# A scan and the subtraction behind it as one step of the plan

## The chip, the cores and the metric

The kernel runs on one core of a Trainium2 chip. The metric is the device time of one execution in microseconds (us), as the median of several runs. The core's engines work side by side, each through its own list of instructions in a fixed order: TensorE (PE in the profile, with PEld for its weight loads), VectorE (DVE), ScalarE (ACT), GpSimd (POOL) and SyncE (SP), which issues most DMAs. They wait for each other through semaphores.

## The reference

The model is a two-layer decoder trunk on 256 tokens of width 1024. Layer 0 is stick-breaking attention with 16 heads of 64, then an MLP with squared ReLU. Layer 1 is sparse attention with shared keys and values, then another such MLP. The change touches the attention of layer 0 alone:

```python
z = jnp.einsum('bqhd,bshd->bhqs', q_blk, k).astype(jnp.float32) * scale
causal = key_pos[None, :] < t[:, None]
log_1m = jnp.where(causal, jax.nn.log_sigmoid(-z), 0.0)
excl = lax.cumsum(log_1m, axis=3, reverse=True) - log_1m
a = jnp.where(causal, jnp.exp(jax.nn.log_sigmoid(z) + excl), 0.0)
return jnp.einsum('bhqs,bshd->bqhd', a.astype(v.dtype), v)
```

The weight of a key is therefore exp(z minus the sum, over this key and all later ones up to the query, of log(1 + exp z)). The sum runs from the last key back to the first.

## The kernel before

The kernel is one long program, written out instruction by instruction. The order of the matmuls on PE is given by hand. The order of the small work on DVE, ACT and POOL is chosen by a planner (class `Order`) while the program is built. It keeps a clock of its own. Each matmul that is written out advances the clock by an assumed cost. Small work is given to it as chains (class `Chain`), generators that yield one step after another. A step is a dictionary from the engines that could do it ("D", "A", "G" for DVE, ACT, POOL) to an assumed cost in ns, the function that issues the instruction, and a flag for a port that DVE and POOL share. When an engine is free by the planner's clock, it takes the step with the lowest rank among those that are ready. The next step of a chain becomes ready 35 ns after the end of the last by that clock, so between two steps of one chain another chain's step can take the engine. What `need` asks for must be planned before the next matmul is written.

Every fp32 weight is split into two parts for PE. ACT casts the raw tile to `wh` (line 422) and DVE subtracts that from it to get `wl` (line 437). A raw tile whose `wl` is done can be loaded anew by SP.

The attention of layer 0 handles eight pairs of heads in four groups g of two pairs. `proj(p)` multiplies the queries and keys of pair p into PSUM tiles `qk`. ACT copies one part to `qku` (1037), DVE adds the other into `qkT` (1038), and DVE or POOL multiplies by the row scale (1040, 1041). `scores(g)` multiplies `qkT` into `z`, in PSUM banks 4 to 7, and starts a chain `soft` for each pair. That chain is:

- DVE caps `z` into `sbe`, two halves (1052);
- ACT takes the exponential (1056) and the logarithm of one plus it (1057) into `sbs`;
- DVE sums `sbs` backwards with a scan (1058);
- DVE subtracts `sbs` from `sbe` (1059);
- ACT takes the exponential of `sbe` (1060).

`turn(g, i, b)` transposes four tiles of 128 by 128 of `sbe` on PE into bank b (`pa`), and ACT or DVE copies them to `sbt` (1097). `values(g, b)` multiplies `sbt` with `v` into `po` in bank b, and `o_evac` brings it to `oT` in two parts: a cast on ACT (649) and a subtraction on DVE (650). `out_part` multiplies `oT` with the output weights into the accumulators `acc`.

PE's order in a group g from 1 on is: a part of `proj(2g+2)` with the transposes of group g-1 in between, `scores(g)`, `values(g-1)`, the rest of `proj(2g+2)` and `proj(2g+3)`. Behind the last of these come `out_part` for the first heads, the transposes of group 2, `scores(3)`, `values(2)`, and further parts of the output projection. `values(2, 1)` puts its `po` in bank 1, and the accumulator `acc11`, which is written next but a few matmuls, takes bank 1 as well.

In this text the groups are counted from 1: group 1 is `scores(0)`, and group 4 is `scores(3)`.

Of the kernel before, what the change touches and what calls it, by code (L numbers as in the profile page):

```python
# [12 lines left out]
OP = mybir.AluOpType  # L13
# [3 lines left out]
D = 1024  # L17
# [148 lines left out]
def act(n, f, more=0):  # L166
    return {"A": (195 + 0.835 * n + more, f, False)}


def dve(n, f, more=0, port=False):  # L170
    return {"D": (150 + 1.045 * n + more, f, port)}
# [7 lines left out]
def hybrid_kernel(ctx, tc, x, xt, eye, gcols, gfin, wqk, wv, wo0, wkv, wvs, wq, wg, wo1, w1, w2, cw1, cw2, cpos, gate_b, consts, out):  # L179
    nc = tc.nc  # L180
# [731 lines left out]
    def layer0(ap):  # L912
# [76 lines left out]
        go_on = ap.tile([P, 2 * ROW], BF16, name="go_on", bufs=1)  # L989
# [56 lines left out]
        def soft(z, got):  # L1046
            e = ap.tile([P, 2 * ROW], F32, name="sbe", bufs=3)
            s = ap.tile([P, 2 * ROW], F32, name="sbs", bufs=2)
            nc.gpsimd.memset(e.rearrange("p (b c) -> p b c", b=6)[:, :, P:SEG], NEG)

            def low(hd):
                return dve(384, lambda: nc.vector.tensor_tensor(
                    e[:, hd * ROW:(hd + 1) * ROW].rearrange("p (b c) -> p b c", b=3)[:, :, 0:P],
                    z[hd][:, 0:384].rearrange("p (b c) -> p b c", b=3), cap, op=OP.min))
            yield [low(0), low(1)]
            yield act(774, lambda: nc.scalar.activation(s, e, AF.Exp))
            yield act(774, lambda: nc.scalar.activation(s, s, AF.Ln, bias=1.0))
            yield dve(774, lambda: nc.vector.tensor_tensor_scan(s[:, ::-1], s[:, ::-1], go_on[:, ::-1], 0.0, OP.add, OP.mult), 810, True)  # L1058
            yield {"D": (956, lambda: nc.vector.tensor_sub(e, e, s), True)}
            yield act(774, lambda: nc.scalar.activation(e, e, AF.Exp))  # L1060
            got.append(e)

        def scores(g):
            zs = [[B(4 + 2 * j + hd, "z") for hd in range(2)] for j in range(2)]
            qks = []
            for j in range(2):
                qkT, ch = live.pop(("q", 2 * g + j))
                o.need(*ch)
                qks.append(qkT)
            o.tick(90)  # L1070
            for j in range(2):
                for hd in range(2):
                    r = slice(hd * DH, (hd + 1) * DH)
                    mm(zs[j][hd][:, 0:256], qks[j][r, 0, P:2 * P], qks[j][r, 1, :], True, False, 2.0)
                for hd in range(2):
                    r = slice(hd * DH, (hd + 1) * DH)
                    mm(zs[j][hd][:, 256:384], qks[j][r, 0, 0:P], qks[j][r, 1, 0:P], False, True, 2.0)
                got = []
                live["e", 2 * g + j] = got, go(soft(zs[j], got), 1 + 0.01 * g)
            o.tick(90)  # L1080
# [893 lines left out]
```

## Time and profile before

| | us |
|---|---|
| median of 3 runs | 591.42 |
| lowest and highest | 591.16, 592.12 |
| the profiled execution | 591.92 |
| its span, first to last instruction | 590.1 |
| PE busy in it | 581.5 |
| DVE busy | 523.6 |
| ACT busy | 433.3 |
| POOL busy | 94.6 |

The profiled execution is one run of the program. The table's busy times are sums over the span. A busy PE is not a PE at its peak, because matmuls are pipelined and their ends are modelled. In rows of the trace the first number is the start in us from the start of the span and the second the duration. A row ending in "x3" holds three such instructions one behind the other. A bracket names the idle time of the engine just before, and whose work ended it.

### The profile page before, as it was taken

Reading aid. Unit: us, or ns where it says so; the run is one execution under the profiler, and the core shown is the slowest. Engines: PE = TensorE matmul, PEld = TensorE weight load, DVE = VectorE, ACT = ScalarE, POOL = GpSimd, SP = SyncE. Lnnn points to the kernel's source line nnn. Section 1 sums busy time; section 2 is a strip of 40 time slices with the busy share of each in tenths; the row PEclk is TensorE's granted clock in tenths of the full one; section 3 lists DMA queues with packets and bytes.
Section 4 is the critical chain, followed back from the end, with each engine's and each line's share of the span. In section 5 each row is a group of like instructions: output and inputs, shape, how many; then the busy total and the mean of one; then the engine's idle time right before and its main releaser. Section 6 shows DMA issues by size and latency. Waiting matters only on the chain.

```text
span 590.1 us, 9338 instructions
## 1 busy us (share of the span) xinstructions
PE 581.5 (99%) x3340; PEld 487.7 (83%) x3340; DVE 523.6 (89%) x842; ACT 433.3 (73%) x704; POOL 94.6 (16%) x114
## 2 busy tenths in 40 slices
PE   9999999999999999999999999999999999999995
PEld 6888887888888888888888878677888888888884
DVE  6679999699999999987895899965999999999976
ACT  6757776588797878783944797572988988887863
POOL 0013220001211212000120443330001121211001
PEclk9999999999999999999999999999999999999998
DMA  8982337179888998544645634323399888987311
GB/s 325 402 283 76 124 127 264 66 236 387 271 207 241 276 293 248 163 140 150 202 165 182 250 110 139 113 107 108 110 366 333 206 271 228 315 256 202 69 37 71
DMA packets 38063, 119.77 MB, mean 203 GB/s; under 512 B 4608, under 2 KB 5888, under 8 KB 38016
## 3 DMA queue, kind: packets, MB, share of 16 engines
q1 hardware_dynamic: 31248, 106.94, 51.1%
q0 software_dynamic: 6336, 11.54, 11.8%
q10 hardware_dynamic: 432, 0.69, 0.3%
q8 instruction: 26, 0.43, 0.3%
q14 instruction: 21, 0.17, 0.1%
HBM read 118.10 MB, written 1.05 MB: 202 GB/s over the span
## 4 chain that ended last, share of the span: by engine, by line
PE 88%; DVE 7%; ACT 4%; issue 1%; POOL 0%; POOLq 0%; ACTq 0%
PE acc L554 32%; PE pu L554 30%; PE pk L554 5%; PE qk L554 4%; PE pv L554 4%; PE qp L554 3%; PE po L554 3%; DVE wl L437 2%; PE z L554 2%; PE ptp L566 2%; DVE sbs L1058 1%; ACT pe L1462 1%; PE ph L554 1%; ACT wh L422 1%; PE pt L566 1%
## 5 line engine op out<-in xcount | busy, mean ns | idle before, releaser
L437 DVE TENSOR_TENSOR wl<-raw,wh 128x1024 fp32r<-128x1024 f32 x128 | 157.4, 1246 | 8.6 <-ACT wh L422 7.7
L422 ACT CAST wh<-raw 128x1024 fp32r<-128x1024 f32 x128 | 132.8, 1054 | 18.3 <-DMA raw<-in_wq 6.9
L554 PE MATMUL pu<-xn,wh 128*128 128x512 f32 x512 | 126.9, 390 | 0.0
L554 PEld LDWEIGHTS pu<-xn,wh 128*128 128x128 f32 x512 | 95.2, 188 | 19.2
L554 PEld LDWEIGHTS pu<-xn,wl 128*128 128x128 f32 x512 | 68.4, 188 | 5.0
L554 PE MATMUL pu<-xn,wl 128*128 128x256 f32 x512 | 69.4, 278 | 0.0
L444 POOL DMA_DIRECT2D fours<-in_w x24 | 22.4, 933 | 196.3 <-DVE ms L802 101.8
L769 ACT COPY mu<-pu 128x512 f32<-128x512 f32 x64 | 37.2, 583 | 16.6 <-PE pu L554 16.1
L554 PE MATMUL acc<-wh,hh 128*128 128x512 f32 (+1 forms) x126 | 49.3, 392 | 0.0
L554 PE MATMUL acc<-wl,hh 128*128 128x512 f32 (+1 forms) x126 | 49.2, 390 | 0.0
L554 PE MATMUL acc<-wh,hl 128*128 128x512 f32 (+1 forms) x126 | 48.8, 387 | 0.0
L554 PE MATMUL acc<-wh,oT 128*128 128x512 f32 x128 | 43.5, 402 | 0.7 <-DVE oT L650 0.7
L554 PE MATMUL acc<-tl,hh 128*128 128x512 f32 x104 | 40.8, 392 | 0.0
L554 PE MATMUL acc<-th,hh 128*128 128x512 f32 x104 | 40.7, 392 | 0.0
L554 PE MATMUL acc<-th,hl 128*128 128x512 f32 x104 | 40.5, 389 | 0.0
L791 DVE TENSOR_TENSOR hl<-ms,hh 128x896 fp32r<-128x896 f32 (+2 forms) x34 | 33.1, 978 | 5.7 <-ACT hh L790 5.7
L785 ACT ACTIVATE ms<-ms 128x512 f32<-128x512 f32 x32 | 20.2, 633 | 24.0 <-DVE ms L784 23.8
L444 POOL DMA_DIRECT2D four<-in_w x20 | 18.9, 946 | 87.3 <-DVE ms L802 13.9
L790 ACT CAST hh<-ms 128x896 fp32r<-128x896 f32 (+2 forms) x34 | 29.0, 854 | 5.1 <-DVE ms L802 3.5
L1462 ACT ACTIVATE pe<-pe,nm 128x256 f32<-128x256 f32 (+1 forms) x64 | 28.5, 450 | 5.7 <-DVE nm L1460 5.7
L554 PE MATMUL pk<-wh,xk 128*128 128x512 f32 (+1 forms) x128 | 32.6, 339 | 0.0
L554 PE MATMUL qk<-xa,wh 128*128 128x512 f32 x128 | 31.2, 393 | 0.0
(229 smaller groups left out, 1239.8 us busy)
## 6 DMA issues: line engine op xcount, KB each, us to landing
raw<-in_w SPq DMA_DIRECT2D x76, 512.0 KB, 7.3
four<-in_w SPq DMA_DIRECT2D x28, 512.0 KB, 7.4
fours<-in_w SPq DMA_DIRECT2D x24, 512.0 KB, 8.2
raw<-in_wqk SPq DMA_DIRECT2D x16, 512.0 KB, 6.2
raw<-in_wo SPq DMA_DIRECT2D x16, 512.0 KB, 4.7
fours<-in_w POOLq DMA_DIRECT2D x24, 256.0 KB, 7.2
four<-in_w POOLq DMA_DIRECT2D x20, 256.0 KB, 6.6
raw<-in_wkv SPq DMA_DIRECT2D x8, 512.0 KB, 3.9
```

Of the source, the lines that this page charges most:

```text
L422: k = {"A": (195 + 0.835 * m, lambda: nc.scalar.copy(a, b), False), "D": (200 + 0.49 * m, lambda: nc.vector.tensor_copy(a, b), True)}
L437: yield {"D": (150 + 1.045 * m, lambda: nc.vector.tensor_sub(lo, raw, f32(hi)), True)}
L444: nc.gpsimd.dma_start(to, other, accum_op=OP.add)
L554: nc.tensor.matmul(o_, a, b, start=first, stop=last, skip_group_check=True)
L566: nc.tensor.transpose(o_, a, i)
L769: yield act(512, lambda: nc.scalar.copy(dst, src))
L785: yield act(512, lambda: nc.scalar.activation(s4f, s4f, AF.Relu))
L790: yield act((b - a) * P, lambda: nc.scalar.copy(hh[:, into], flat[:, q]))
L791: yield dve((b - a) * P, lambda: nc.vector.tensor_sub(hl[:, into], flat[:, q], f32(hh[:, into])), port=True)
L1058: yield dve(774, lambda: nc.vector.tensor_tensor_scan(s[:, ::-1], s[:, ::-1], go_on[:, ::-1], 0.0, OP.add, OP.mult), 810, True)
L1462: act(n, lambda: nc.scalar.activation(d, d, AF.Exp, bias=nm[:, i:i + 1], scale=-1.0, accum_out=rs[:, t, hd, b:b + 1]), 150)]
```

## The change

In `soft`, the scan and the subtraction were two steps, so the planner could put other work on DVE between them. Now one step issues both, and DVE's instructions stand back to back.

```diff
-            yield dve(774, lambda: nc.vector.tensor_tensor_scan(s[:, ::-1], s[:, ::-1], go_on[:, ::-1], 0.0, OP.add, OP.mult), 810, True)
-            yield {"D": (956, lambda: nc.vector.tensor_sub(e, e, s), True)}
+
+            def weigh():
+                nc.vector.tensor_tensor_scan(s[:, ::-1], s[:, ::-1], go_on[:, ::-1], 0.0, OP.add, OP.mult)
+                nc.vector.tensor_sub(e, e, s)
+            yield {"D": (956 + 1750, weigh, True)}
```

The assumed costs were 150 + 1.045 x 774 + 810 = 1769 ns and 956 ns; the new step has 2706 ns. The planner makes other choices behind it, all within the attention of layer 0. From the residual addition behind it to the end of the program, every engine has the same instructions in the same order as before, and PE and SP have so throughout. Over the program DVE loses three copies to `sbt` (ACT has them) and gains two products `qkT` (POOL loses them). From here on, line 1058 becomes 1060, 1059 becomes 1061, and what follows moves by three lines.

The first place is DVE in group 2, from the scores of that group to the weights behind it. Before:

```order
L650 TENSOR_TENSOR oT<-po,oT 128x512
L1058 SCALAR_TENSOR_TENSOR sbs<-sbs,go_on 128x774
L1038 TENSOR_TENSOR qkT<-qk,qku 128x256 x2
L1040 TENSOR_TENSOR qkT<-qkT,rbq 128x256
L1059 TENSOR_TENSOR sbe<-sbe,sbs 128x774
L1058 SCALAR_TENSOR_TENSOR sbs<-sbs,go_on 128x774
L1038 TENSOR_TENSOR qkT<-qk,qku 128x256
L1059 TENSOR_TENSOR sbe<-sbe,sbs 128x774
L1038 TENSOR_TENSOR qkT<-qk,qku 128x256
L437 TENSOR_TENSOR wl<-raw,wh 128x1024
L1097 COPY sbt<-pa 128x512
L437 TENSOR_TENSOR wl<-raw,wh 128x1024 x3
```

The same place in the changed kernel, where the scan is listed as L1060 and the subtraction as L1061:

```order
L1060 SCALAR_TENSOR_TENSOR sbs<-sbs,go_on 128x774
L1061 TENSOR_TENSOR sbe<-sbe,sbs 128x774
L650 TENSOR_TENSOR oT<-po,oT 128x512
L1038 TENSOR_TENSOR qkT<-qk,qku 128x256 x2
L1040 TENSOR_TENSOR qkT<-qkT,rbq 128x256
L1060 SCALAR_TENSOR_TENSOR sbs<-sbs,go_on 128x774
L1061 TENSOR_TENSOR sbe<-sbe,sbs 128x774
L1038 TENSOR_TENSOR qkT<-qk,qku 128x256 x2
L1040 TENSOR_TENSOR qkT<-qkT,rbq 128x256
L437 TENSOR_TENSOR wl<-raw,wh 128x1024 x4
```

The pair stands together, `oT` has moved from ahead of the first scan to behind the first subtraction, a second product L1040 has come, and the copy L1097 has gone. Group 3 is the same, but that it had no copy on DVE before and has three `wl` instead of four. In group 1 the copy has gone as well, and no product has come.

The second place is ACT around the first logarithm of group 2. Before:

```order
L1097 COPY sbt<-pa 128x512 x2
L1056 ACTIVATE sbs<-sbe 128x774
L649 CAST oT<-po 128x512
L1057 ACTIVATE sbs<-sbs 128x774
L1037 COPY qku<-qk 128x256 x2
```

The same place in the changed kernel, where the copy to `sbt` is listed as L1100:

```order
L1100 COPY sbt<-pa 128x512 x3
L1056 ACTIVATE sbs<-sbe 128x774
L1057 ACTIVATE sbs<-sbs 128x774
L649 CAST oT<-po 128x512
L1037 COPY qku<-qk 128x256
```

The logarithm has moved ahead of the cast of `oT`, and ACT makes all three copies. Group 3 has the first of these two as well.

The third place is DVE in group 4, where `oT` holds the attention output of group 3. Before:

```order
L1052 TENSOR_TENSOR sbe<-z,cst 128x3x128 x4
L437 TENSOR_TENSOR wl<-raw,wh 128x1024
L1058 SCALAR_TENSOR_TENSOR sbs<-sbs,go_on 128x774
L650 TENSOR_TENSOR oT<-po,oT 128x512
L1059 TENSOR_TENSOR sbe<-sbe,sbs 128x774
L1058 SCALAR_TENSOR_TENSOR sbs<-sbs,go_on 128x774
```

The same place in the changed kernel:

```order
L1052 TENSOR_TENSOR sbe<-z,cst 128x3x128 x4
L437 TENSOR_TENSOR wl<-raw,wh 128x1024
L1060 SCALAR_TENSOR_TENSOR sbs<-sbs,go_on 128x774
L1061 TENSOR_TENSOR sbe<-sbe,sbs 128x774
L650 TENSOR_TENSOR oT<-po,oT 128x512
L1060 SCALAR_TENSOR_TENSOR sbs<-sbs,go_on 128x774
```

The subtraction has moved ahead of `oT`.

## The prediction

> **What bounds the kernel.** I read the busy shares first, then what TensorE (PE) waits for, then the chain of waits around the changed lines, then VectorE's (DVE's) instructions there in order of time. The first view gives each engine's busy time and share of the span:
>
> ```profile
> PE 581.5 (99%) x3340; PEld 487.7 (83%) x3340; DVE 523.6 (89%) x842; ACT 433.3 (73%) x704; POOL 94.6 (16%) x114
> ```
>
> PE has almost no idle time, and the change leaves its matmuls and their order as they are. So the time moves only where PE's few waits move. The list of waits (who, for whom, total us, times, longest) has two for another engine's work, in the whole span:
>
> ```profile
> PE acc L554 <- DVE oT L650: 0.7, 1, 0.7
> PE ptp L566 <- ACT pe L1462: 0.7, 1, 0.7
> ```
>
> The second lies in layer 1, which the change does not touch. The first is in the attention of layer 0, and the chain of waits (start, us, what) passes through it, with DVE ahead of it:
>
> ```profile
> 90.68 1.13 DVE wl L437
> 91.81 1.68 DVE sbs L1058
> 93.49 0.59 DVE oT L650
> 94.09 0.04 issue
> 94.13 6.46 PE acc L554 x27
> ```
>
> This is the output projection: its accumulator `acc11` takes PSUM bank 1, which still holds the attention output `po` of group 3 until DVE has read it for `oT` (L650). PE goes on 0.05 us after DVE's `oT` ends. **So the question is when that `oT` ends**, and ahead of it DVE works nearly without a pause. These are DVE's instructions from the second group's scores on, in order of time (start, duration, engine, line, operation, tiles):
>
> ```profile
> 58.42 1.94 DVE L1052 TENSOR_TENSOR sbe<-z,cst 128x384 f32<-128x384 f32 x4
> 60.88 0.69 DVE L650 TENSOR_TENSOR oT<-po,oT 128x512 fp32r<-128x512 f32 x1 [0.52 <-ACT oT L649]
> 61.63 1.77 DVE L1058 TENSOR_TENSOR_SCAN sbs<-sbs,go_on 128x774 f32<-128x774 f32 x1
> 63.32 0.73 DVE L1038 TENSOR_TENSOR qkT<-qk,qku 128x256 f32<-128x256 f32 x2
> 64.08 0.74 DVE L1040 TENSOR_TENSOR qkT<-qkT,rbq 128x256 f32<-128x256 f32 x1
> 64.74 0.95 DVE L1059 TENSOR_TENSOR sbe<-sbe,sbs 128x774 f32<-128x774 f32 x1
> 65.62 1.76 DVE L1058 TENSOR_TENSOR_SCAN sbs<-sbs,go_on 128x774 f32<-128x774 f32 x1
> 67.30 0.39 DVE L1038 TENSOR_TENSOR qkT<-qk,qku 128x256 f32<-128x256 f32 x1
> 67.62 0.95 DVE L1059 TENSOR_TENSOR sbe<-sbe,sbs 128x774 f32<-128x774 f32 x1
> 68.49 0.41 DVE L1038 TENSOR_TENSOR qkT<-qk,qku 128x256 f32<-128x256 f32 x1
> 68.82 1.43 DVE L437 TENSOR_TENSOR wl<-raw,wh 128x1024 fp32r<-128x1024 f32 x1
> 70.17 0.68 DVE L1097 COPY sbt<-pa 128x512 f32<-128x512 f32 x1
> 70.78 3.48 DVE L437 TENSOR_TENSOR wl<-raw,wh 128x1024 fp32r<-128x1024 f32 x3
> 74.18 1.94 DVE L1052 TENSOR_TENSOR sbe<-z,cst 128x384 f32<-128x384 f32 x4
> ...
> 84.59 4.23 DVE L437 TENSOR_TENSOR wl<-raw,wh 128x1024 fp32r<-128x1024 f32 x3
> 88.74 1.94 DVE L1052 TENSOR_TENSOR sbe<-z,cst 128x384 f32<-128x384 f32 x4
> 90.61 1.21 DVE L437 TENSOR_TENSOR wl<-raw,wh 128x1024 fp32r<-128x1024 f32 x1
> 91.74 1.75 DVE L1058 TENSOR_TENSOR_SCAN sbs<-sbs,go_on 128x774 f32<-128x774 f32 x1
> 93.42 0.66 DVE L650 TENSOR_TENSOR oT<-po,oT 128x512 fp32r<-128x512 f32 x1
> 94.00 0.95 DVE L1059 TENSOR_TENSOR sbe<-sbe,sbs 128x774 f32<-128x774 f32 x1
> ```
>
> What one instruction takes of DVE is the step to the next start: the scan 1.69 (61.63 to 63.32), the subtraction 0.88 (64.74 to 65.62), `oT` 0.58 (93.42 to 94.00), the copy L1097 0.61, a `wl` 1.13 (3.40 for three from 70.78).
>
> **The change, part by part.** I follow one landmark, the L1052 rows that open each group (58.42, 74.18 and 88.74 for groups 2, 3 and 4), and then `oT` of the stall.
>
> *The pair itself.* An instruction that does not need the one in front starts 0.08 us before that one's end: the scan ends at 61.63 + 1.77 = 63.40, and L1038 starts at 63.32. One that reads the result in front starts 0.03 after it: L1038 x2 ends at 64.05, L1040 starts at 64.08. The subtraction reads what the scan wrote, so a pair costs 1.77 + 0.03 = 1.80 where the scan now takes 1.69: **+0.11 a pair**, and seven pairs stand ahead of the stall, 0.77 in all. [...]
>
> *Group 1, up to 58.42.* DVE's copy L1097 goes to ACT (0.61 less); two pairs add 0.22. The third thing is POOL, which multiplies `qkT` (L1041) there three times:
>
> ```profile
> 48.60 1.40 POOL L1041 TENSOR_TENSOR qkT<-qkT,rbq 128x256 f32<-128x256 f32 x1 [8.13 <-DVE qkT L1038]
> 49.30 2.32 DVE L1058 TENSOR_TENSOR_SCAN sbs<-sbs,go_on 128x774 f32<-128x774 f32 x1
> 52.09 3.01 POOL L1041 TENSOR_TENSOR qkT<-qkT,rbq 128x256 f32<-128x256 f32 x2 [2.09 <-DVE qkT L1038]
> 53.06 1.43 DVE L437 TENSOR_TENSOR wl<-raw,wh 128x1024 fp32r<-128x1024 f32 x1
> 54.42 0.68 DVE L1097 COPY sbt<-pa 128x512 f32<-128x512 f32 x1
> 63.80 0.74 POOL L1041 TENSOR_TENSOR qkT<-qkT,rbq 128x256 f32<-128x256 f32 x1 [8.62 <-DVE qkT L1038]
> ```
>
> POOL takes 0.74 when DVE leaves it alone and up to twice that among DVE's long instructions, which stretch too: the scan to 2.32 (0.55 more than 1.77), the `wl` to 1.36 from start to start (0.23 more). One of the three costs nothing now, since DVE reads PSUM meanwhile (the copy at 54.42). Without that copy all three fall among scan, subtraction and `wl`. Bounds: no more than now (0), or three times 0.74 less the 0.78 paid now (+1.44). I take a third collision at the mean of the two seen, +0.39. Sum: -0.61 + 0.22 + 0.39 = **0.0**, between -0.39 and +1.05.
>
> *Group 2, 58.42 to 74.18.* On ACT the logarithm now comes ahead of the cast of `oT`:
>
> ```profile
> 59.53 0.85 ACT L1056 ACTIVATE sbs<-sbe 128x774 f32<-128x774 f32 x1 [2.44 <-DVE sbe L1052]
> 60.75 0.85 ACT L1057 ACTIVATE sbs<-sbs 128x774 f32<-128x774 f32 x1
> ...
> 90.73 0.85 ACT L1057 ACTIVATE sbs<-sbs 128x774 f32<-128x774 f32 x1
> ```
>
> From L1052 to the scan it is 3.21 now (58.42 to 61.63, 0.03 behind the logarithm's end); in group 4, where the logarithm is not held up, its end is 91.58, and with the same 0.03 it is 2.87 from 88.74: -0.34. DVE's `oT` stood in that gap, where DVE waited for the logarithm anyway; it now follows the first subtraction, in full work: +0.58. Two L1038 come together and the second product goes from POOL to DVE: 0.66 for it (64.08 to 64.74) and 0.11 for a second dependent start. Two pairs: +0.22. The copy leaves: -0.61. The `wl` that collided with POOL (68.82 to 70.17, 1.35) is free: -0.22. Sum **+0.40**.
>
> *Group 3, 74.18 to 88.74.* The same -0.34 + 0.58 + 0.77 + 0.22, no copy to lose, and the three `wl` (84.59 to 88.74, 4.15) back to 3.40, since one POOL product is gone: -0.75. Sum **+0.48**.
>
> *Group 4, to the stall.* Before, `oT` slipped in between scan and subtraction. Now it stands behind the pair: 0.87 (94.00 to the next scan, read as for the others) and the 0.11: **+0.98**.
>
> Together 0.0 + 0.40 + 0.48 + 0.98 = **+1.86**: `oT` ends at 95.94 instead of 94.08 and PE goes on 1.86 later. Nothing behind gives it back: PE has no other wait but the one of 0.7 in layer 1, which follows PE's own matmuls. What the added work delays besides is hidden: the last copy to `sbt` moves to ACT, behind PE's transposes, which come 1.86 later too (uncovered it would cost its 0.61); `wl` of the next weights comes up to 2 us later, as PE does; the loads on SP's queue that these free keep their order. The profiled execution took 591.92 (span 590.1), so 593.78; it lay 0.50 above the median of the three runs, 591.42, hence **593.3**.
>
> **Rivals.** *The backlog does not build up.* If groups 2 and 3 cost DVE no more (the collisions that go pay for `oT` and the products), only the step in group 4 is left: +0.98, so 592.4. For it speak the `wl` rows at 68.82 and 84.59, which show nearly 1 us of collisions to be won; against it that both are in the sum already.
>
> *The wait goes instead.* ACT takes three copies off DVE and each exponential starts sooner. PE's last matmul before the stall starts at 93.00, the next could at 93.23:
>
> ```profile
> 93.00 0.39 PE L554 MATMUL acc<-wh,oT 128*128 128x512 f32 x1
> 94.13 0.50 PE L554 MATMUL acc<-wh,oT 128*128 128x512 f32 x1 [0.74 <-DVE oT L650]
> ```
>
> If `oT` ended by then, 0.90 would be won: 590.5, not slower. It decides at 93.18 for the end of `oT`; that needs the L1052 of group 4 at 86.9, 1.8 us earlier than now, while my sum has it 0.88 later.
>
> *More than the sum.* With group 1 at its upper end (+1.05) the exponentials of groups 2 and 3 come late for PE's transposes too, but `oT` still decides: +2.9, 594.3.
>
> *PE loses its clock.* PE would stand from 93.23 to 96.0, 2.8 us, the longest gap in this stage. The granted clock is at its full value in every slice:
>
> ```profile
> PEclk9999999999999999999999999999999999999998
> ```
>
> If the 27 matmuls behind the gap (6.46) ran at half speed, it would be up to 6.5 more, 599.8. [...] No run here shows such a gap yet.
>
> **How the numbers follow.** Forecast +1.9: 0.71. Backlog does not build up: 0.16. The wait goes: 0.05. More than the sum: 0.05. Clock: 0.03. About 0.2% (1.2 us) is what a measurement of this kernel tells from no change. The forecast with its bounds and the last two are beyond it but for a few hundredths; the first rival lies within, and the second too (0.90 is 0.15%), with 0.03 left for more than I see. So faster 0.03, same 0.20, slower 0.77. The range runs from just under the first rival, 592.2, to the upper end of group 1, 594.4.
>
> **What would show it.** Right: the L1052 rows of groups 3 and 4 at about 74.6 and 89.6, `oT` of group 4 ending near 95.9, PE's wait for it at about 2.6 instead of 0.7, every later PE row shifted alike. Scan and subtraction should start 1.80 apart. Wrong: L1052 of group 4 at 88.7 or earlier; PE waiting for exponentials or copies instead; a `PEclk` below full; or a later wait of PE that shrinks by the same amount.

## The result and the profile after

| | median us | lowest to highest | runs |
|---|---|---|---|
| before | 591.56 | 591.16 to 592.12 | 6 |
| changed | 595.52 | 594.28 to 596.73 | 6 |

The ratio is 1.0065, with a 95% interval of 1.005 to 1.0079. The kernel became slower by 4.0 us, and its runs lie further apart than those before. The sign was forecast. The size was not: 595.52 lies above the range. The profiled execution is the quickest of the six, 594.28 with a span of 592.5.

On its page, PE's work is what it was, and its share of the span is lower:

```profile
span 592.5 us, 9352 instructions
...
PE 581.5 (98%) x3340; PEld 487.6 (82%) x3340; DVE 523.5 (88%) x841; ACT 434.8 (73%) x707; POOL 90.6 (15%) x112
```

The list of PE's waits (who, for whom, total us, times, longest) shows where the difference is. The wait for `oT` has grown from 0.7 to 2.7, and a small one for an exponential is new:

```profile
PE acc L554 <- DVE oT L650: 2.7, 1, 2.7
PE warm L554 <- PEq L1967: 0.8, 1, 0.8
PE ptp L566 <- ACT pe L1465: 0.6, 1, 0.6
PE pa L566 <- ACT sbe L1063: 0.3, 1, 0.3
```

The chain of waits around it now has the subtraction ahead of `oT`:

```profile
94.94 0.96 DVE sbe L1061
95.90 0.61 DVE oT L650
96.51 0.04 issue
96.56 6.46 PE acc L554 x27
```

DVE in order of time, first the capping of group 1, then group 2, then what opens groups 3 and 4 and leads to `oT`:

```profile
43.16 1.95 DVE L1052 TENSOR_TENSOR sbe<-z,cst 128x384 f32<-128x384 f32 x4 [1.55 <-PE z L554]
...
58.32 1.94 DVE L1052 TENSOR_TENSOR sbe<-z,cst 128x384 f32<-128x384 f32 x4
61.20 1.77 DVE L1060 TENSOR_TENSOR_SCAN sbs<-sbs,go_on 128x774 f32<-128x774 f32 x1 [0.94 <-ACT sbs L1057]
63.07 0.97 DVE L1061 TENSOR_TENSOR sbe<-sbe,sbs 128x774 f32<-128x774 f32 x1
63.95 0.69 DVE L650 TENSOR_TENSOR oT<-po,oT 128x512 fp32r<-128x512 f32 x1
64.55 0.75 DVE L1038 TENSOR_TENSOR qkT<-qk,qku 128x256 f32<-128x256 f32 x2
65.33 0.74 DVE L1040 TENSOR_TENSOR qkT<-qkT,rbq 128x256 f32<-128x256 f32 x1
65.99 1.76 DVE L1060 TENSOR_TENSOR_SCAN sbs<-sbs,go_on 128x774 f32<-128x774 f32 x1
67.85 0.96 DVE L1061 TENSOR_TENSOR sbe<-sbe,sbs 128x774 f32<-128x774 f32 x1
68.73 0.75 DVE L1038 TENSOR_TENSOR qkT<-qk,qku 128x256 f32<-128x256 f32 x2
69.52 0.79 DVE L1040 TENSOR_TENSOR qkT<-qkT,rbq 128x256 f32<-128x256 f32 x1
70.23 4.62 DVE L437 TENSOR_TENSOR wl<-raw,wh 128x1024 fp32r<-128x1024 f32 x4
74.77 1.94 DVE L1052 TENSOR_TENSOR sbe<-z,cst 128x384 f32<-128x384 f32 x4
...
90.08 1.94 DVE L1052 TENSOR_TENSOR sbe<-z,cst 128x384 f32<-128x384 f32 x4
91.94 1.21 DVE L437 TENSOR_TENSOR wl<-raw,wh 128x1024 fp32r<-128x1024 f32 x1
93.08 1.76 DVE L1060 TENSOR_TENSOR_SCAN sbs<-sbs,go_on 128x774 f32<-128x774 f32 x1
94.94 0.96 DVE L1061 TENSOR_TENSOR sbe<-sbe,sbs 128x774 f32<-128x774 f32 x1
95.82 0.68 DVE L650 TENSOR_TENSOR oT<-po,oT 128x512 fp32r<-128x512 f32 x1
```

The same row of group 1 in the kernel before:

```profile
43.35 1.95 DVE L1052 TENSOR_TENSOR sbe<-z,cst 128x384 f32<-128x384 f32 x4 [1.55 <-PE z L554]
```

From landmark to landmark the two profiles give:

| stretch | before | after | more | forecast |
|---|---|---|---|---|
| L1052 of group 1 to group 2 | 15.07 | 15.16 | 0.09 | 0.0 |
| group 2 to group 3 | 15.76 | 16.45 | 0.69 | 0.40 |
| group 3 to group 4 | 14.56 | 15.31 | 0.75 | 0.48 |
| group 4 to the end of `oT` | 5.34 | 6.42 | 1.08 | 0.98 |
| sum | | | 2.61 | 1.86 |

So the later `oT` explains 2.6 us, which from 591.56 gives 594.2. That is the time of the profiled execution, but 1.3 us short of the median. (From the start of the span, PE's restart moved by 2.43, from 94.13 to 96.56, since group 1 opens 0.19 earlier in the profile after.)

### The profile page after: what moved, and what is told of

Read it like the earlier page. It is cut to its first block, busy times and chain, and to the rows that moved or that the text cites. A ratio compares the mean times of both kernels' runs of the same rounds, so it can differ in the third digit from the quotient of the medians.

```text
span 592.5 us, 9352 instructions
## 1 busy us (share of the span) xinstructions
PE 581.5 (98%) x3340; PEld 487.6 (82%) x3340; DVE 523.5 (88%) x841; ACT 434.8 (73%) x707; POOL 90.6 (15%) x112
## 4 chain that ended last, share of the span: by engine, by line
PE 84%; DVE 9%; ACT 5%; issue 1%; DMA 1%; POOL 0%; POOLq 0%; DVEq 0%; ACTq 0%
PE acc L554 32%; PE pu L554 30%; PE pk L554 4%; PE pv L554 4%; PE qp L554 3%; PE po L554 3%; PE qk L554 2%; DVE wl L437 2%; DVE sbs L1060 2%; ACT pe L1465 2%; PE ptp L566 1%; PE z L554 1%; ACT wh L422 1%; DVE sbe L1061 1%; PE ph L554 1%; PE pt L566 1%
## 5 line engine op out<-in xcount | busy, mean ns | idle before, releaser
L554 PEld LDWEIGHTS acc<-wh,oT 128*128 128x128 f32 x128 | 24.0, 188 | 9.0 <-DVE oT L650 3.2
```

The costliest lines, as they stand in the source:

```text
L554: nc.tensor.matmul(o_, a, b, start=first, stop=last, skip_group_check=True)
```

## The experiments

Two theories stood against each other. By **A**, this delay of `oT` (DVE's backlog) is all, and the rest is scatter. By **B**, PE's granted clock (the share of its full speed that it may run at) drops for a while behind the long wait, in some executions. Each run also lists its mean granted clock over the whole execution: in the first six runs of the changed kernel 0.998 for the two quickest and 0.995 for the other four. The mean alone is a weak sign, since the traces also end at half clock, behind PE's last matmul (3.2 us of it in the kernel before, from 586.9 to 590.1, 2.6 in the changed one, from 589.9 to 592.5, and about 4.3 in after_late below), and the kernel before has 0.996 to 0.999 with 591 to 593 us. The kernel before took 591.78 beside the first four kernels below and 591.89 beside the next four; the ratios are against these.

**The changed kernel again.** No edit.

> The changed kernel once more. Theory A (DVE's backlog alone makes the time): every run near 594.2, that is 591.56 + 2.6, the shift of PE's restart between the two profiles; what lies above is scatter. Theory B (besides the backlog, PE's granted clock drops for a while behind the 3 us wait, in some executions): two kinds of runs, mean clock 0.998 with 594.3 to 594.7, and 0.995 with 595.3 to 596.7; a profile of the second kind shows a granted clock below 1 in the stretch behind PE's wait for oT and longer matmuls there.

595.57 (594.52 to 597.16), ratio 1.0062 (1.0049 to 1.0075). At 0.998 it took 594.55 and 594.52, at 0.996 or less 595.41 to 597.16. The profiled one was again of the first kind, with a wait of 2.7.

**Matmuls in the wait.** Their result is read by nothing.

```diff
+        fill = B(4, "fill")
+        for i in range(10):
+            nc.tensor.matmul(fill, nc.const_aps.tensor(1.0, [P, P], BF16), nc.const_aps.tensor(1.0, [P, 512], BF16), start=True, stop=True, skip_group_check=True)
         out_part(oT, acc, i_o0, 1, (0, 1, 2, 3))
```

> The changed kernel with ten matmuls 128x512 into bank 4, whose result nothing reads, placed in PE's wait for oT (about 2.2 us of its 2.9); DVE, ACT, POOL and SP have the same order. Theory A: no change against the changed kernel, 595.5 with the same scatter. Theory B: PE is no longer idle there, so the mean clock is 0.998 in every run and the time 594.3, with 1 us less scatter.

594.34 (593.81 to 594.74), ratio 1.0041 (1.0029 to 1.0053): 1.2 us quicker than the changed kernel by ten matmuls more. The mean clock is 0.996 to 0.998, not 0.998 in every run as B had it; in the trace of 594.34, with 0.997, the row `PEclk` has 9 in every slice but the last, which has 8. PE, in order of time, with the ten (one record is missing) ahead of the last three matmuls before the wait:

```profile
92.92 2.36 PE L1150 MATMUL fill<-const-bfloat16-1.0 128*128 128x512 bf16 x9
94.92 0.58 PE L554 MATMUL acc<-wh,oT 128*128 128x512 f32 x1
95.35 0.40 PE L554 MATMUL acc<-wl,oT 128*128 128x512 f32 x1
95.58 0.40 PE L554 MATMUL acc<-wh,oT 128*128 128x512 f32 x1
96.50 0.50 PE L554 MATMUL acc<-wh,oT 128*128 128x512 f32 x1 [0.52 <-DVE oT L650]
```

PE goes on at 96.50, as in the changed kernel (96.56). Only the idling has gone, and with it the upper runs. Theory A expected no change here.

**The wait reached later.** The matmuls of `acc01` come ahead of those of `acc11`.

```diff
-        out_part(oT, acc, i_o0, 1, (0, 1, 2, 3))
+        out_part(oT, acc, i_o0, 1, (0, 1, 2, 3), ts=(0,))
+        out_part(oT, acc, i_o0, 1, (0, 1, 2, 3), ts=(1,))
```

> The changed kernel, with the twelve matmuls of acc01 ahead of the twelve of acc11 instead of three and three in turn; nothing else moves. PE reaches its wait for oT nine matmuls later, 9 x 0.228 = 2.05 us, so a wait of about 0.9 is left. Theory A: 595.5 - 2.05 = 593.5. Theory B: the short wait does not cost clock either, 594.3 - 2.05 = 592.2, with clock 0.998 in every run.

592.17 (591.75 to 592.76), ratio 1.0008 (0.9999 to 1.0016). That is B's number, 592.2, and 3.4 us below the changed kernel, though only 2.05 us of waiting were taken away. PE's wait is 0.7. Here too the mean clock, 0.996 to 0.999, is not 0.998 in every run, and the trace (0.996) has 1.00 in all stretches from 0 to 575 us and 0.86 in the last 15.5.

**Group 4 split again.** The pair stands in groups 1 to 3 alone; `soft` is given `g` for that.

```diff
-            yield {"D": (956 + 1750, weigh, True)}
+            if g < 3:
+                yield {"D": (956 + 1750, weigh, True)}
+            else:
+                yield dve(774, lambda: nc.vector.tensor_tensor_scan(s[:, ::-1], s[:, ::-1], go_on[:, ::-1], 0.0, OP.add, OP.mult), 810, True)
+                yield {"D": (956, lambda: nc.vector.tensor_sub(e, e, s), True)}
```

> The changed kernel, with scan and subtraction as two steps again in group 4 alone (g == 3): oT stands between them again, DVE's backlog from groups 1 to 3 stays. oT ends about 1.08 earlier and PE's wait is 1.8 instead of 2.9. Theory A: 595.5 - 1.1 = 594.4. Theory B: with a wait of 1.8 the clock stays, 594.3 - 1.1 = 593.2; if the clock still drops, the runs are of two kinds again.

593.10 (592.77 to 594.16), ratio 1.0023 (1.0014 to 1.0032). PE's wait is 1.6, and the row `PEclk` has 9 in every slice, the one behind the wait too. The backlog of groups 1 to 3 alone costs 1.3 us, as B had it.

**A wait without the pair.** The kernel before, with operations ahead of that `oT` on DVE (`live["hold"]` is a piece of the row scale, 128 by 400, and is set for that one `oT` alone):

```diff
+                for i in range(3 if p0 == 4 and live.get("hold") is not None else 0):
+                    nc.vector.tensor_tensor(live["hold"], live["hold"], live["hold"], op=OP.max)
                 nc.vector.tensor_sub(lo, src, f32(hi))
```

> The kernel before, with three DVE operations (maximum of the row scale rbq with itself, 400 columns, in place) ahead of the oT that PE waits for; nothing else moves, so scan and subtraction stay apart. They take about 3 x 0.67 = 2.0 us, so PE stands for about 2.9 us as in the changed kernel. Theory A (only the wait itself costs): 591.8 + 2.0 = 593.8 in every run. Theory B (the granted clock drops behind a wait of 2.9 us in some executions): runs at 593.8 with clock 0.997 or more, others 1 to 2.5 above at 0.996 or less, median 594.9.

594.69 (593.12 to 595.10), ratio 1.0037 (1.0023 to 1.005). The three took 1.68 us instead of 2.0. Two runs with 0.998 took 593.12 and 593.18, three with 0.995 or 0.996 took 594.69 to 595.10. So a longer wait gives two kinds of runs by itself, with scan and subtraction apart. The profiled run is one of the three. A stretch of 1 us (columns: start to end, length, then busy time of PE, PEld, DVE, ACT, POOL with counts, granted clock, DMA share, GB/s), and the row with which PE goes on:

```profile
95.00:96.00 1.00, 0.14 (x1) 0.14 (x1) 1.00 (x3) 0.59 (x1) 0.00 (x0) 0.71 1.01 410
```

```profile
95.86 0.80 PE L554 MATMUL acc<-wh,oT 128*128 128x512 f32 x1 [2.42 <-DVE oT L656]
```

A mean of 0.71 over a stretch that ends 0.14 us behind PE's restart means that the clock was already low while PE waited. The next two stretches of 1 us have 0.50; at that clock it was low from about 95.4, an estimate from the 0.71. The first matmul takes 0.80 where it takes 0.50 in the changed kernel's profile.

**The same with five.** The loop has 5 in place of 3.

> The same with five such operations, 3.35 us, so PE stands for 4.2 us. Theory A: 591.8 + 3.35 = 595.1 with the scatter of the kernel before (about 1 us from lowest to highest of five). Theory B: every run drops, 595.1 + 1.7 = 596.8 or more, mean clock 0.995 or less, and the profile shows a granted clock below 1 behind the wait and matmuls of twice the duration.

596.15 (596.04 to 597.59), ratio 1.0081 (1.0069 to 1.0094). The five took 2.90 us instead of 3.35, and PE's wait was 3.6. With 2.90, A's sum is 594.8 and B's 596.5. All five runs have 0.992 to 0.996. Three stretches of its profile, in the same columns:

```profile
92.70:96.70 4.00, 0.36 (x3) 0.00 (x1) 3.86 (x8) 2.52 (x3) 0.00 (x0) 1.00 0.93 348
96.70:97.90 1.20, 1.20 (x5) 1.02 (x6) 1.20 (x2) 0.35 (x1) 0.00 (x0) 1.00 0.59 242
97.90:101.40 3.50, 3.50 (x10) 2.69 (x10) 3.50 (x4) 0.68 (x2) 0.00 (x0) 0.51 0.06 13
```

PE waits at full granted clock, works 1.2 us at full clock, and only then runs at half clock, for about 3.4 us (a mean of 0.51 over 3.50).

**The pair in group 4 alone.** The condition of the split is `g == 3` in place of `g < 3`, so groups 1 to 3 have two steps as before.

> The kernel before, with scan and subtraction as one step in group 4 alone. The backlog of groups 2 and 3 is not there; oT comes behind the pair, about 1.06 later (0.88 for the subtraction and 0.18 for its start 0.10 behind the scan's end instead of 0.08 ahead of it). Theories A and B: PE's wait is 1.8 to 2.0, too short for the clock, 591.8 + 1.06 = 592.8. If the backlog of groups 2 and 3 were not a cost of its own, this would be near the changed kernel, 595.5.

593.00 (592.30 to 594.26), ratio 1.0018 (1.0009 to 1.0027), with a wait of 1.8: the expected 592.8, within the scatter. Its lower runs have 592.3 to 592.7. Five runs with a mean clock of 0.996 took 593.0 to 594.3, but one with 0.999 took 593.7. The profile, of 592.30, has a granted clock of 1.00 from 93 to 100, so whether a wait of 1.8 sometimes costs clock stays open.

This kernel's 1.1 us and the 1.3 us of groups 1 to 3 are 2.4 together. The change that has both costs 3.8 to 4.0.

**The order of the accumulators in the kernel before.** The same edit as for the wait reached later.

> The kernel before, with the twelve matmuls of acc01 ahead of the twelve of acc11. PE reaches bank 1 2.05 us later and oT has long ended, so the wait of 0.74 (0.90 from start to start) goes: 591.8 - 0.9 = 590.9 by both theories. If something else held PE at that place, 591.8.

590.98 (590.57 to 591.25), ratio 0.9984 (0.9976 to 0.9993). The wait for `oT` is gone from PE's list. This version is quicker than both kernels.

**Two more executions of the changed kernel**, for a profile of one with the lower clock.

> The changed kernel, one profiled execution, to catch one with the lower mean clock. Theory B: with a mean clock of 0.995 the profile shows about 3.4 us of half clock that begin during or right behind PE's wait for oT, near 95 to 97, and the span is about 594.2; with 0.998 it is 592.6 and no such stretch. Theory A: no stretch of lower clock near 96 in either case.

594.73 with 0.998: the clock was full throughout the stretch from 93 to 102. Its wait for `oT` is 2.8.

> The same again, since about one execution in three keeps the clock: the same two outcomes.

595.73 with 0.995. Its wait for `oT` is 2.8. Its stretches of 1 us behind the wait, in the columns of the stretches above, and PE's rows around it:

```profile
95.00:96.00 1.00, 0.00 (x0) 0.00 (x0) 1.00 (x2) 1.00 (x2) 0.00 (x0) 1.00 1.04 414
96.00:97.00 1.00, 0.76 (x3) 0.67 (x4) 1.00 (x2) 1.00 (x2) 0.00 (x0) 0.93 0.98 401
97.00:98.00 1.00, 1.00 (x3) 0.76 (x3) 0.90 (x2) 0.41 (x1) 0.00 (x0) 0.50 1.05 430
98.00:99.00 1.00, 1.00 (x4) 0.75 (x3) 1.00 (x2) 0.03 (x1) 0.00 (x0) 0.50 0.43 172
99.00:100.00 1.00, 1.00 (x4) 0.81 (x3) 1.00 (x2) 0.82 (x2) 0.00 (x0) 0.50 0.05 20
100.00:101.00 1.00, 1.00 (x5) 0.77 (x5) 1.00 (x2) 1.00 (x1) 0.00 (x0) 0.87 0.00 0
101.00:102.00 1.00, 1.00 (x6) 0.83 (x5) 1.00 (x2) 0.05 (x1) 0.00 (x0) 1.00 0.77 213
```

```profile
93.08 0.39 PE L554 MATMUL acc<-wh,oT 128*128 128x512 f32 x1
96.24 0.50 PE L554 MATMUL acc<-wh,oT 128*128 128x512 f32 x1 [2.77 <-DVE oT L650]
...
98.05 1.05 PE L554 MATMUL acc<-wh,oT 128*128 128x512 f32 x2
98.90 0.63 PE L554 MATMUL acc<-wl,oT 128*128 128x512 f32 x1
```

PE idles from 93.47 to 96.24. Then the clock is at half from about 96.9 to 100.3, and a pair of matmuls that otherwise starts the next one 0.46 us later takes 0.85 (98.05 to 98.90). The clock that is missing adds up to 0.07 + 3 x 0.50 + 0.13 = 1.70 us. The execution before had the same wait and lost none. From its restart to the start of the sixth matmul with `wl`, PE took 3.80 us there (96.73 to 100.53) and 5.37 here (96.24 to 101.61): 1.57 us more. With this theory A falls: the lower clock is in the trace of the changed kernel itself.

The drop does not begin at the same point of the wait: at about 95.4 in hold3, 0.4 us ahead of PE's restart at 95.86; at 96.9 in after_look2, 0.6 behind 96.24; at 97.9 in hold5, 1.2 behind 96.70. By the stretches of 1 us the missing clock is 0.29 + 2 x 0.50 + 0.41 = 1.70 us in hold3 (95 to 99), 1.70 in after_look2 and 0.03 + 3 x 0.50 + 0.18 = 1.71 in hold5 (97 to 102), so each spent 3.4 us at half clock. The waits were 2.42, 2.77 and 3.64. after_again and after_look1 waited 2.74 and 2.76 and kept the clock. Why one execution loses it and the next does not is not shown: no run placed the wait on purpose.

## Why the prediction was wrong

**What bounds the kernel** held. PE's wait for `oT` in bank 1 is the place; other stalls of PE hardly moved (0.3 us for an exponential of group 3, which the wait for `oT` absorbs). Putting off PE's arrival (before_late) wins 0.9 us, as it should, so the reading of the bank is shown.

**The pair** had the right mechanism and the wrong size. The prediction took 0.03 us from end to start, from L1038 and L1040. Scan and subtraction show 0.10 (the scan ends at 61.20 + 1.77 = 62.97, the subtraction starts at 63.07), so a pair costs 0.18 more, not 0.11. Over seven pairs that is 0.5 of the 0.75 us by which the backlog was sized too small.

**Group 1** came out near the forecast, 0.09 for 0.0, in part by luck, since two errors cancel. The two pairs cost 0.36, not 0.22. The collisions with POOL cost DVE 1.06, where 0.78 + 0.39 = 1.17 was assumed (POOL's products take 2.13 from 49.49 and 3.25 for two from 52.92, against 0.74 at 65.05), and they fall on other instructions: a subtraction takes 1.18 to the next start (51.19 to 52.37) instead of 0.88, and three `wl` take 4.16 (54.16 to 58.32) instead of 3.40.

**Groups 2 and 3** lost what was said, in the way it was said. From L1052 to the scan it is 2.88 (forecast 2.87), the three `wl` of group 3 take 3.40 (90.08 - 86.68), as forecast. The pairs make 0.14 of the 0.29 and 0.27 that each has beyond the forecast; the rest is 0.02 to 0.05 on several rows, such as 0.71 from the second product to `wl` (69.52 to 70.23) where 0.66 was used.

**Group 4**, 1.08 for 0.98, is the subtraction (0.88) and the 0.18 of a pair. The run pair4 shows it alone, with 1.1.

**The rival on the clock is the step that failed.** It was given 0.03, and no run stood behind that. PE's gap was 2.8, and the clock still halved for 3.4 us, by trace in after_look2, and in hold3 and hold5 with another cause of the wait. By the mean clock, nine of fourteen executions of the changed kernel had it: 595.75 in the median, against 594.55 for the five that kept 0.998. In after_look2 the missing clock is 1.70 us. The 1.7 in the expectation of hold5 was the author's estimate, shown by no run at that time. The bound of 6.5 us by the 27 matmuls was far too wide, since in all three traces the slow stretch ended after 3.4 us, while they still ran. The row of `PEclk` was misread as well: its last slice is 8, not 9.

**The sum**, then: 1.86 should have been 2.6, and about 1.2 is missing for the clock in the median. 591.6 + 2.6 + 1.2 = 595.4, for 595.5 measured. Without the clock the time would have been 594.3 (after_fill: 594.34), only just within the stated range. So two terms failed: the pair, sized at 0.11 instead of 0.18, makes most of what the backlog lacks, and the clock, left out of the sum, takes the time out of the range. The 1.2 is read from the runs, as the difference of the two medians; why it is less than the 1.57 us of the trace stays open.

**The other rivals.** The backlog did build up: split4 has 1.3 us of it by itself. The wait did not go. *More than the sum* came near in size, 2.6 against 2.9, but not in the way it was given, since group 1 stayed at 0.09.

## What to carry to other kernels

Making two dependent steps one removes the work that stood between them, and it shifts everything that the planner placed by the gap; look for the small instruction behind it that frees a buffer for the busiest engine. A wait of TensorE can cost clock besides its own length: here 1.7 us in after_look2, with a wait of 2.77, and none in after_look1, with 2.76. So look at the granted clock behind a wait of that length, and time several executions. If the wait can't go, try independent matmuls in it, which won 1.2 us here (after_fill). Here a change of the order of two accumulators removed the wait in the kernel before and nearly all the loss in the changed one.

## What the runs showed of the hardware

- At PE's wait for `oT` and behind it the granted clock was 0.50 for 3.4 us in the traces of hold3 (wait 2.42), after_look2 (2.77) and hold5 (3.64). It stayed at 1.00 in after_look1 (2.76; from 95 to 102 us) and in the first profile of the changed kernel (2.74; from 93.4 to 130 us). By the mean clock, 12 of the 19 runs of hold3 and the changed kernel had the drop, and all five of hold5. With waits of 0.5 to 0.7 (before, after_fill, after_late), 1.6 (split4) and 1.8 (pair4) no profile shows it at this place.
- The lower clock did not begin with the wait's end: in hold3 it began 0.4 us before PE went on, in after_look2 0.6 and in hold5 1.2 us after. No run shows what sets that moment.
- In the changed kernel's profile a subtraction that reads what a scan wrote started 0.10 us behind the scan's end (62.97 to 63.07). In the profile before, a product that reads what an addition wrote started 0.03 behind it (64.05 to 64.08). Three operations in place on one tile took 1.76 us together in hold3, from the first start to the last end, where 2.0 was expected.
